# One pool of four PSUM banks in place of three small pools, in a two-layer hybrid streaming trunk on one Trainium2 core

## The chip, the cores and the metric

The kernel runs as one program on one NeuronCore of a Trainium2 chip. The metric is device time in microseconds (us), the median of several executions; lower is better. The engines are named as the profile names them: PE is TensorE (its weight loads are listed apart as PEld), DVE is VectorE, ACT is ScalarE, POOL is GpSimd and SP is SyncE, which issues most of the DMAs. A `q` behind an engine's name means its instruction sequencer.

## The reference

Two layers of a hybrid block work on a prompt of 512 tokens and on a decode group of 32 tokens that share the same weights. Cut to what matters:

```python
h = rms_norm(x, g_mix)
glu_a, glu_b, rq, rk, rv, rg, fq, fk, fv, ff, gates = split_in(h @ w_in)
u = glu_a * sigmoid(glu_b)                                # branch A: causal conv over 31 taps
y_conv = silu(layer_norm(dwconv(up, w_dw_conv) + b_dw_conv)) @ w_conv_out
o, new_ret = retention_chunks(rotary(rq), rotary(rk), rv, ret_state)     # branch B, 8 heads
y_ret = (silu(rg) * group_norm(o)) @ w_ret_out
fq, fk = rms_norm(fq, g_q_fox), rms_norm(fk, g_k_fox)     # branch C, 8 heads of 64
s = fq @ fk.T / 8 + cum_q - cum_k                         # cum: cumulative log forget gate
y_fox = (softmax(where(causal, s, -inf)) @ fv) @ w_fox_out
x = x + (sig(gA) * y_conv + sig(gB) * y_ret + sig(gC) * y_fox) @ w_out
x = x + (gelu(dwconv3(rms_norm(x) @ W_a)) * (rms_norm(x) @ W_b)) @ W_down
```

## The kernel before

All activations are held transposed, 128 channels on the partitions and 544 tokens (32 of the decode group, then 512 of the prompt) along the free side. Every projection is a `gemm` (line 296): eight or more weight blocks of 128x128, streamed from HBM and split by ACT and a POOL-issued DMA into a high and a low part (`Stream.split_part`, lines 201 to 215), are multiplied with two halves of 272 tokens (line 314). A gemm accumulates in one tile `acc` of the pool `psA`, which has two buffers of two banks each, and DVE then evicts it (lines 403, 1040, 1042, 1162, 1203 and others). A new gemm can begin in a bank pair only when the gemm before the last one has been evicted.

The other four banks hold small tiles. Before the change they are three pools: `psS` with two banks (name `s`: scores, head means, sums over channels, transposes of the values), `psT` with one bank (`t`: transposes and the state products of the retention), and `psO` with one bank (`o`: products of probabilities and values). PE writes such a tile, and DVE or ACT reads it out; the bank can be written again when its last reader is done. Nothing else in the change's neighbourhood is shared.

The order of the work is written by hand. A "side" generator (attention in `fox_side`, retention in `ret_side`, group norm in `gn_side`) is advanced at fixed places between the blocks of each gemm (`hook`, `tick`), and the 27 multiply-adds of the depthwise convolution (`conv_side`, line 511, each a DVE instruction of about 0.8 us) are dealt out in the same ticks from `extra`. Each engine executes its instructions in order, so a DVE instruction stands behind the convolution steps that were put ahead of it.

Per layer the sequence is: gates and values of the convolution, q and k of the attention with their head means (`head_mean`, lines 345 and 346, read by `rsqrt`, lines 357 to 362), the value projection with its transposes (lines 648 and 650), then the decode group's scores for two groups of four heads (`s_scores`, line 718, read by DVE at line 729; `s_trans`, line 736, read by ACT at lines 740 and 741), then 16 pairs of prompt scores (`p_scores`, line 771: the even and the odd head's products stand in two `s` tiles and are read by DVE at line 778; softmax at lines 704 to 709; `p_trans`, line 786, read by ACT at line 789; `p_pv`, line 805). The retention follows with five chunks (lines 886 to 939; the state update reads its `t` tile on DVE at line 933 or 937).

Of the kernel before, what the change touches and what calls it, by code (L numbers as in the profile page):

```python
# [11 lines left out]
F32 = mybir.dt.float32  # L12
# [5 lines left out]
P = 128  # L18
# [94 lines left out]
def trunk(ctx, tc, x_in, wpack, wff, consts, params, s_conv, s_ret, s_cache, s_clf, s_ffn,  # L113
          y_out, o_conv, o_ret, o_fk, o_fv, o_lf, o_ffn):
    nc = tc.nc
    PS = bass.MemoryType.PSUM
# [11 lines left out]
    upool = ctx.enter_context(tc.tile_pool(name="upool", bufs=3))  # L128
    dpool = ctx.enter_context(tc.tile_pool(name="dpool", bufs=2, space=bass.MemoryType.DRAM))
    psA = ctx.enter_context(tc.tile_pool(name="psA", bufs=2, space=PS))  # L130
    psS = ctx.enter_context(tc.tile_pool(name="psS", bufs=2, space=PS))
    psT = ctx.enter_context(tc.tile_pool(name="psT", bufs=1, space=PS))
    psO = ctx.enter_context(tc.tile_pool(name="psO", bufs=1, space=PS))

    def Q(dt=F32):
        return qpool.tile([P, 4, T], dt, tag="q", name="q")
# [13 lines left out]
        return ap.rearrange("p (h n) -> p h n", h=2)  # L150

    def psS_t():
        return psS.tile([P, 512], F32, tag="s", name="s")

    def psT_t():
        return psT.tile([P, 512], F32, tag="t", name="t")

    def psO_t():
        return psO.tile([P, 512], F32, tag="o", name="o")


    cst = cpool.tile([P, C_ALL], F32, name="cst")
# [172 lines left out]
    def head_mean(src):  # L335

        hi, lo = Wr(), Wr()
        act(hi, src, AF.Copy)  # L338
        vtt(lo, src, hi.bitcast(F32), op=ALU.subtract)  # L339

        def product():
            res = []
            for h in range(2):
                p = psS_t()[:, :HN]
                mm(p, blkr, half(hi, h), start=True, stop=False)
                mm(p, blkr, half(lo, h), start=False, stop=True)
                res.append(p)
            return res

        return product  # L350
# [13 lines left out]
    class Norm:  # L364
# [26 lines left out]
        def finish(self):  # L391
            self.R = spool.tile([P, T], F32, tag="R", name="R", bufs=1)
            parts = [psS_t()[:, :HN] for _ in range(2)]
            for h, p in enumerate(parts):
                mm(p, ones, half(self.ss, h), start=True, stop=True)
            rsqrt(self.R, parts, D)
# [16 lines left out]
    adma = nc.scalar.dma_start  # L413

    junk = psT_t()
    for _ in range(10):
        mm(junk[:, 0:P], ones, ones, start=True, stop=True)
# [35 lines left out]
    for l in range(DEPTH):  # L453
# [90 lines left out]

        def logf_1():
            t = psT_t()
            for b in range(4):
                nc.tensor.transpose(t[:, b * 64 : b * 64 + 64], zf[0:64, NS + b * P : NS + (b + 1) * P],
# [35 lines left out]
        def logf_2():  # L584
            dma(o_lf[l], LG)
            t = psT_t()
            lg = LG.rearrange("p h b -> p (h b)")
            mm(t[:, 0:56], tri, lg, start=True, stop=True)
            mm(t[:, 64:120], ones, lg, start=True, stop=True)
            tot = t[:, 64:120].rearrange("p (h b) -> p h b", b=NB)  # L590
            pf = spool.tile([P, 8, NB], F32, tag="pf", name="pf", bufs=1)
            nc.vector.memset(pf, 0.0)
            for b in (1, 2, 3, 5, 6):
                vtt(pf[:, :, b], tot[:, :, b - 1], pf[:, :, b - 1], op=ALU.add)
            vtt(CM, t[:, 0:56].rearrange("p (h b) -> p h b", b=NB), pf, op=ALU.add)
# [42 lines left out]
        def v_done(vt, vs, j, out):  # L638
            def done(acc):
                v = Wt()  # L640
                R_norm.evict(v, acc)

                def fin():
                    if out is not None:
                        dma(out[:, j, :], v)
                    t = psS_t()
                    for b in range(4):
                        nc.tensor.transpose(t[:, b * P : (b + 1) * P], v[:, NS + b * P : NS + (b + 1) * P], ident)  # L648
                    s = psT_t()
                    nc.tensor.transpose(s[:, 0:P], v[:, 0:P], ident)  # L650
                    act(vt[:, :, j * P : (j + 1) * P], t.rearrange("p (b n) -> p b n", b=4), AF.Copy)
                    act(vs[0:NS, j * P : (j + 1) * P], s[0:NS, 0:P], AF.Copy)

                after(fin, 2)

            return done
# [22 lines left out]
        def fox_side():  # L679
# [64 lines left out]
            def s_pv(it):  # L744
                g = it["g"]
                pt = it["pt"]
                o = psO_t()
                for pr in range(2):
                    for b in range(3):
                        for e in range(2):  # L750
                            i = pr * 2 + e
                            h = g * 4 + i
                            kk = P if b < 2 else NS
                            vv = vc[:, b, h * 64 : h * 64 + 64] if b < 2 else fvs[0:NS, h * 64 : h * 64 + 64]
                            mm(o[e * 64 : e * 64 + 64, pr * NS : (pr + 1) * NS], vv,
                               pt[0:kk, b * P + i * NS : b * P + (i + 1) * NS], start=(b == 0), stop=(b == 2))
                src = o[:, 0 : 2 * NS].rearrange("p (a n) -> p a n", a=2)
                hl_split(foh[:, 2 * g : 2 * g + 2, 0:NS], fol[:, 2 * g : 2 * g + 2, 0:NS], src)
# [35 lines left out]
            def p_pv(it):  # L794
                h, qb = it["h"], it["qb"]
                if h % 2 == 0:
                    it["mate"]["even"] = it
                    return
                ev = it["even"]
                if qb == 0:  # L800
                    obank[0] = psO_t()
                o = obank[0]
                for b in range(qb + 1):
                    for e, x in ((0, ev), (1, it)):
                        mm(o[e * 64 : e * 64 + 64, qb * P : (qb + 1) * P], fv[:, b, (h - 1 + e) * 64 : (h + e) * 64],  # L805
                           x["pt"][:, b * P : (b + 1) * P], start=(b == 0), stop=(b == qb))
                if qb == 3:
                    hl_split(foh[:, h // 2, NS:T], fol[:, h // 2, NS:T], o)
# [67 lines left out]
        def ret_side():  # L876
# [5 lines left out]
            for c0, c, n in chunks:  # L882
# [25 lines left out]
                yield  # L908
                yield
                o = psO_t()  # L910
                kv = psT_t()

# [408 lines left out]
```

## Time and profile before

| | us |
|---|---|
| median of three runs (1975.41 to 1976.87) | 1976.23 |
| the profiled execution | 1979.67 |
| its span, from the first to the last instruction of the program | 1977.9 |
| PE busy in it | 1944.8 |
| DVE busy | 946.0 |
| ACT busy | 1065.0 |
| POOL busy | 412.6 |

The profiled execution is 3.4 us above the median, and 1.8 us of it lie outside the span. PE is busy in nearly all of it, DVE and ACT in about half, but these are averages over stages: attention and retention lie at about 120 to 345 us in the first layer and 1100 to 1330 us in the second, and the rest is mostly dense gemms.

### The profile page before, as it was taken

To read this page: it belongs to the slowest core of one execution; us is meant where nothing else is said; L and a number is where in the kernel's file an instruction comes from. 1 tells how busy PE (TensorE), PEld (TensorE's weight loads), DVE (VectorE), ACT (ScalarE), POOL (GpSimd) and SP (SyncE) were. 2 spreads that over 40 slices of the span, in tenths; PEclk is the share of its full clock that TensorE was granted. 3 is DMA by queue.
4 is the path that set the end of the run, shared out by engine and by line. 5 is a ranking of instruction groups with operands and counts; after the bars stand their busy time and mean duration, and the time that the engine had idled before them with its cause. 6 is when DMAs were issued, how large, how long until landed. Compare 5 with 4: busy or idle time off the path is not lost.

```text
span 1977.9 us, 37772 instructions
## 1 busy us (share of the span) xinstructions
PE 1944.8 (98%) x15852; PEld 1903.0 (96%) x15852; DVE 946.0 (48%) x1642; ACT 1065.0 (54%) x1467; POOL 412.6 (21%) x573
## 2 busy tenths in 40 slices
PE   9999999999999999999999999999999999999999
PEld 8998899999999999999999987999999999999999
DVE  4486988454334330333225869784534343203320
ACT  7566663665455543455446566536654555434542
POOL 1243422121112221221112343211211122112211
PEclk9999999999999999999999999999999999999999
DMA  8786555667888787888887765647678878877786
GB/s 254 179 208 158 129 129 123 146 156 168 197 195 176 174 177 176 176 175 180 212 203 153 205 145 129 139 110 154 151 176 198 195 174 175 177 177 173 176 182 143
DMA packets 106005, 337.39 MB, mean 171 GB/s; under 512 B 17788, under 2 KB 19436, under 8 KB 105580
## 3 DMA queue, kind: packets, MB, share of 16 engines
q0 software_dynamic: 41616, 151.54, 46.0%
q1 hardware_dynamic: 64076, 183.44, 28.0%
q8 instruction: 124, 2.03, 0.4%
q14 instruction: 45, 0.37, 0.1%
q10 hardware_dynamic: 144, 0.00, 0.0%
HBM read 320.59 MB, written 9.89 MB: 167 GB/s over the span
## 4 chain that ended last, share of the span: by engine, by line
PE 80%; DVE 9%; issue 4%; ACT 4%; DMA 2%; SPq 1%; POOL 1%; DVEq 0%; POOLq 0%; ACTq 0%
PE acc L314 76%; DVE w L511 4%; DMA w<-q 1%; DVE w L778 1%; ACT hi L207 1%; DVE mn L704 1%; ACT lo L210 1%; PE o L805 1%; DVE w L779 1%; SPq L834 0%; DVE q L838 0%; PE s L771 0%; PE t L786 0%; DMA q<-in_wpack_dram 0%; PE s L648 0%
## 5 line engine op out<-in xcount | busy, mean ns | idle before, releaser
L314 PE MATMUL acc<-q,hi 128*128 128x272 f32 x9344 | 1781.7, 290 | 5.6 <-DVE q L333 2.0
L314 PEld LDWEIGHTS acc<-q,hi 128*128 128x128 f32 x9344 | 1470.7, 189 | 19.7 <-issue 7.2
L314 PE MATMUL acc<-q,lo 128*128 128x272 f32 x4672 | 1347.7, 289 | 0.1
L314 PEld LDWEIGHTS acc<-q,lo 128*128 128x128 f32 x4672 | 880.1, 189 | 0.9 <-DMA lo<-in_wpack_dram 0.6
L207 ACT ACTIVATE hi<-raw 128x1024 fp32r<-128x1024 f32 (+1 forms) x292 | 308.7, 1057 | 657.1 <-PE acc L314 656.1
L211 POOL DMA_DIRECT2D lo<-in_wpack_dram x289 | 250.1, 865 | 1273.7 <-ACT lo L210 1236.7
L210 ACT ACTIVATE lo<-hi 128x1024 fp32r<-128x1024 f32 x289 | 304.1, 1052 | 4.5
L511 DVE SCALAR_TENSOR_TENSOR w<-w,par 128x574 f32<-128x574 f32 x208 | 201.2, 967 | 3.7
L1203 DVE TENSOR_TENSOR q<-acc,q 128x544 f32<-128x544 f32 x32 | 23.2, 725 | 218.6 <-PE acc L314 218.6
L403 DVE TENSOR_TENSOR w<-acc,R 128x544 f32<-128x544 f32 x94 | 67.7, 720 | 121.5 <-PE acc L314 119.9
L1162 DVE TENSOR_TENSOR w<-acc,R 128x32 f32<-128x32 f32 x44 | 8.5, 192 | 154.0 <-PE acc L314 153.8
L1170 DVE SCALAR_TENSOR_TENSOR w<-w,par 128x546 f32<-128x546 f32 x44 | 34.7, 789 | 83.5 <-ACT w L1169 83.5
L1172 ACT ACTIVATE w<-w 128x546 f32<-128x546 f32 x44 | 29.1, 662 | 70.6 <-DVE w L1171 70.5
L706 ACT ACTIVATE w<-w,mn 128x128 f32<-128x128 f32 (+4 forms) x68 | 37.8, 556 | 34.9 <-DVE mn L704 31.9
L330 DVE TENSOR_TENSOR q<-w,q 128x544 fp32r<-128x544 f32 x44 | 31.9, 725 | 33.6 <-ACT q L329 33.6
L709 ACT ACTIVATE w<-w,rs 128x128 f32<-128x128 f32 (+4 forms) x68 | 37.8, 556 | 16.8 <-DVE rs L708 16.6
L339 DVE TENSOR_TENSOR wr<-w,wr 128x544 fp32r<-128x544 f32 x24 | 26.0, 1084 | 42.5 <-ACT wr L338 42.5
L518 POOL TENSOR_TENSOR w<-w 128x574 f32<-128x574 f32 x24 | 41.5, 1730 | 17.9 <-ACT w L514 16.5
L1042 DVE SCALAR_TENSOR_TENSOR w<-w,acc 128x544 f32<-128x544 f32 x32 | 23.1, 721 | 43.5 <-PE acc L314 43.2
L361 DVE SCALAR_TENSOR_TENSOR w<-s,w 128x272 f32<-128x272 f32 (+1 forms) x60 | 23.6, 435 | 39.5 <-ACT w L358 39.0
L778 DVE SCALAR_TENSOR_TENSOR w<-ck,CM,s 128x128 f32<-128x128 f32 (+3 forms) x64 | 34.3, 536 | 12.7 <-PE s L771 12.7
L1169 ACT ACTIVATE w<-w,par 128x546 f32<-128x546 f32 x44 | 36.5, 830 | 3.4 <-DVE w L1164 3.4
(206 smaller groups left out, 1414.1 us busy)
## 6 DMA issues: line engine op xcount, KB each, us to landing
raw<-in_wpack_dram SPq DMA_DIRECT2D x290, 512.0 KB, 3.4
lo<-in_wpack_dram POOLq DMA_DIRECT2D x289, 512.0 KB, 5.5
w<-in_x_dram SPq DMA_DIRECT2D x16, 272.0 KB, 4.8
out_dram<-w SPq DMA_DIRECT2D x16, 272.0 KB, 4.5
w<-q SPq DMA_DIRECT2D x64, 68.0 KB, 3.7
ck<-cscr SPq DMA_DIRECT2D x16, 256.0 KB, 4.6
xn<-q SPq DMA_DIRECT2D x8, 272.0 KB, 5.4
w<-xn SPq DMA_DIRECT2D x8, 272.0 KB, 5.8
```

The costliest lines, as they stand in the source:

```text
L207: act(hi[:, sl], self.raw[u][:, sl], AF.Copy)
L210: act(lo[:, sl], hi[:, sl].bitcast(F32), AF.Copy, scale=-1.0)
L211: nc.gpsimd.dma_start(lo[:, sl], wpack[u][:, sl], accum_op=ALU.add)
L314: mm(acc[:, h, :HN], w, half(x, h), start=(i == 0 and j == 0), stop=(i == n - 1 and j == len(passes) - 1))
L403: vtt(two(out), acc, two(self.R), op=ALU.mult)
L511: stt(c, u[:, k : k + CO], pcol(w + k), c, op0=ALU.mult, op1=ALU.add)
L518: gtt(p, p, t, op=ALU.add)
L706: act(L[:, :n], L[:, :n], AF.Exp, scale=-1.0, bias=mn, accum_out=sm)
L709: act(L[:, :n], L[:, :n], AF.Copy, scale=rs)
L778: stt(L[:, :n], c[:, :n], CM[:, h, qb : qb + 1], p[:, :n], op0=ALU.subtract, op1=ALU.subtract)
L1169: act(c, a[:, 0:FO], AF.Identity, scale=pcol(w), bias=pcol(P_FB + j))
L1170: stt(c, a[:, 1 : 1 + FO], pcol(w + 1), c, op0=ALU.mult, op1=ALU.add)
```

## The change

The three pools become one pool `psB` with four buffers, so the number of banks stays at eight. Each small tile takes whichever of the four banks the allocation at build time gives it, instead of a bank of its own kind. No instruction is added or removed.

```diff
     psA = ctx.enter_context(tc.tile_pool(name="psA", bufs=2, space=PS))
-    psS = ctx.enter_context(tc.tile_pool(name="psS", bufs=2, space=PS))
-    psT = ctx.enter_context(tc.tile_pool(name="psT", bufs=1, space=PS))
-    psO = ctx.enter_context(tc.tile_pool(name="psO", bufs=1, space=PS))
+    psB = ctx.enter_context(tc.tile_pool(name="psB", bufs=4, space=PS))
@@
     def psS_t():
-        return psS.tile([P, 512], F32, tag="s", name="s")
+        return psB.tile([P, 512], F32, tag="b", name="s")
     def psT_t():
-        return psT.tile([P, 512], F32, tag="t", name="t")
+        return psB.tile([P, 512], F32, tag="b", name="t")
     def psO_t():
-        return psO.tile([P, 512], F32, tag="o", name="o")
+        return psB.tile([P, 512], F32, tag="b", name="o")
```

The file has two lines less, so a line number of the changed kernel is two below that of before. The order of instructions on POOL and SP is unchanged, on ACT and DVE three and two pairs of neighbours change places, and on PE eight short pieces move by a few instructions. What changes is what PE waits for. First place: PE in the first layer, from the decode scores of the second head group to the first pair of prompt scores, before:

```order
L718 MATMUL s<-q,w 32x256 [waits DVE_49]
L718 MATMUL s<-q,w 32x256 x3
L724 MATMUL s<-w 32x32 [waits Pool_49]
...
L771 MATMUL s<-q 128x256 [waits DVE_49]
L771 MATMUL s<-q 128x256 [waits Activation_49]
L771 MATMUL s<-q 128x256 x4
```

and in the changed kernel:

```order
L716 MATMUL s<-q,w 32x256 [waits Activation_49]
L716 MATMUL s<-q,w 32x256 x3
L722 MATMUL s<-w 32x32 [waits Pool_49]
...
L769 MATMUL s<-q 128x256 [waits DVE_49] x2
L769 MATMUL s<-q 128x256 x4
```

The decode scores of the second group no longer wait for DVE's reading of the first group's scores but for an older ACT copy; the prompt scores behind them now wait for DVE in both banks. Second place: PE in the first layer, where the second decode transposes stand among the second pair of prompt scores, before:

```order
L771 MATMUL s<-q 128x256 [waits DVE_49]
L771 MATMUL s<-q 128x256 x2
L314 MATMUL acc<-q,hi 128x272
L736 MATMUL t<-cst,w 128x128 [waits PE_49,Activation_49]
L737 MATMUL t<-cst,w 128x128
L738 MATMUL t<-cst,w 32x128
L771 MATMUL s<-q 128x256 [waits DVE_49]
L771 MATMUL s<-q 128x256 x2
```

and in the changed kernel:

```order
L734 MATMUL t<-cst,w 128x128 [waits Activation_49]
L735 MATMUL t<-cst,w 128x128
L736 MATMUL t<-cst,w 32x128 [waits DVE_49]
L769 MATMUL s<-q 128x256 [waits DVE_49]
L769 MATMUL s<-q 128x256 [waits DVE_49,PE_49]
L769 MATMUL s<-q 128x256 x4
```

The transposes stand ahead of all six score products, and their bank is another one than that of the first decode transposes. Third place: PE in the retention of the first layer, at its second chunk, where `t` are the transposed keys, before:

```order
L892 MATMUL s<-q 128x128 [waits PE_49] x2
L892 MATMUL s<-q 128x128 x5
L886 MATMUL t<-cst,q 128x128 [waits DVE_49]
L886 MATMUL t<-cst,q 128x128 x3
L892 MATMUL s<-q 128x128
```

and in the changed kernel:

```order
L884 MATMUL t<-cst,q 128x128 [waits PE_49]
L884 MATMUL t<-cst,q 128x128 x3
L890 MATMUL s<-q 128x128
L890 MATMUL s<-q 128x128 [waits Activation_49]
L890 MATMUL s<-q 128x128 x6
```

The transposed keys stand first and no longer wait for DVE.

## Rows read from the trace of the kernel before

**Rows 1.** The page's first lines: span; busy time, share and instructions of each engine.
```profile
span 1977.9 us, 37772 instructions
...
PE 1944.8 (98%) x15852; PEld 1903.0 (96%) x15852; DVE 946.0 (48%) x1642; ACT 1065.0 (54%) x1467; POOL 412.6 (21%) x573
```
**Rows 2.** The page's chain that ended last, shares of the span by line.
```profile
PE acc L314 76%; DVE w L511 4%; DMA w<-q 1%; DVE w L778 1%; ACT hi L207 1%; DVE mn L704 1%; ACT lo L210 1%; PE o L805 1%; DVE w L779 1%; SPq L834 0%; DVE q L838 0%; PE s L771 0%; PE t L786 0%; DMA q<-in_wpack_dram 0%; PE s L648 0%
```
**Rows 3.** Waits of PE, whole span: us in total, times, longest us.
```profile
PE s L771 <- DVE w L778: 4.4, 6, 1.4
PE t L786 <- ACT w L789: 3.9, 5, 1.4
PE s L718 <- DVE w L729: 2.8, 2, 2.4
PE s L345 <- DVE w L361: 2.8, 2, 1.4
PE s L648 <- DVE w L361: 2.8, 2, 2.1
...
PE t L886 <- DVE st L937: 1.9, 4, 0.8
...
PE t L736 <- ACT w L741: 1.4, 1, 1.4
```
**Rows 4.** Stretches in which DVE is full: length, busy us (instructions) by engine, clock, DMA.
```profile
121.00:157.00 36.00, 31.52 (x262) 30.44 (x264) 35.16 (x44) 18.47 (x26) 12.88 (x12) 0.99 0.96 248
...
200.00:249.00 49.00, 43.49 (x351) 38.02 (x348) 47.67 (x87) 31.35 (x65) 20.23 (x15) 1.00 0.52 121
...
1102.00:1139.00 37.00, 33.12 (x262) 31.96 (x264) 36.12 (x45) 18.48 (x26) 12.59 (x12) 0.95 0.85 236
...
1186.00:1231.00 45.00, 41.57 (x336) 36.41 (x334) 45.00 (x84) 28.53 (x60) 16.55 (x14) 1.00 0.55 130
```
**Rows 5.** Stretches of lower granted clock; columns as in rows 4, the clock third from last.
```profile
157.00:160.00 3.00, 3.00 (x25) 2.47 (x22) 1.66 (x6) 2.34 (x7) 0.00 (x0) 0.50 0.88 194
421.00:427.00 6.00, 4.93 (x25) 4.72 (x26) 2.77 (x4) 2.69 (x4) 1.70 (x2) 0.72 0.52 119
1150.00:1153.00 3.00, 3.00 (x13) 2.87 (x13) 1.85 (x5) 1.92 (x7) 1.41 (x2) 0.50 0.90 144
```
**Rows 6.** Timeline, layer one: start us, length us, instruction, [idle before <-releaser].
```profile
149.16 0.72 DVE L403 TENSOR_TENSOR w<-acc,R 128x544 f32<-128x544 f32 x1
...
151.38 0.52 PE L314 MATMUL acc<-q,hi 128*128 128x272 f32 x2
...
156.28 0.51 DVE L729 SCALAR_TENSOR_TENSOR w<-w,cqs,s 128x288 f32<-128x288 f32 x1
...
156.84 1.08 PE L718 MATMUL s<-q,w 64*32 64x256 f32 x8 [2.40 <-DVE w L729]
...
158.09 0.51 DVE L729 SCALAR_TENSOR_TENSOR w<-w,cqs,s 128x288 f32<-128x288 f32 x1 [0.59 <-PE s L724]
...
161.30 0.62 PE L771 MATMUL s<-q 64*128 64x256 f32 x6
```
**Rows 7.** Timeline, the same places in layer two.
```profile
1139.54 0.52 DVE L729 SCALAR_TENSOR_TENSOR w<-w,cqs,s 128x288 f32<-128x288 f32 x1
...
1141.84 0.62 PE L771 MATMUL s<-q 64*128 64x256 f32 x6
...
1147.40 0.33 DVE L778 SCALAR_TENSOR_TENSOR w<-ck,CM,s 128x128 f32<-128x128 f32 x1
...
1149.00 0.33 PE L736 MATMUL t<-cst,w 128*128 128x128 f32 x1 [1.39 <-ACT w L741]
...
1149.48 0.72 PE L771 MATMUL s<-q 64*128 64x256 f32 x3
```
**Rows 8.** Timeline, layer one, end of the full stretch in the attention.
```profile
248.98 0.33 DVE L778 SCALAR_TENSOR_TENSOR w<-ck,CM,s 128x128 f32<-128x128 f32 x1
...
250.28 0.62 PE L771 MATMUL s<-q 64*128 64x256 f32 x6
```

## The prediction, made before the changed kernel was run

> **What bounds the kernel now.** I read the page first. PE is busy for 1944.8 of 1977.9 us [rows 1], so all its idle time is 33.1 us, and a change that adds and removes no instruction can win little more than that. The chain that ended last is mostly PE's gemms, but 4% of it, some 79 us, are the convolution steps of DVE at line 511 [rows 2]. A chain that runs through line 511 says that there are stretches in which DVE, not PE, sets the pace. I then read who waited for whom on PE, to see how much of the idle time is a wait for one of the four small banks, and after that the windows, to see whether DVE was full where these waits stand.
>
> The waits for a small bank's last reader are these [rows 3]: prompt scores 4.4, prompt transposes 3.9, decode scores 2.8, head means 2.8, value transposes 2.8, key transposes of the retention 1.9, decode transposes 1.4. Together 20.0 us, about 1% of the span. PE's other waits are for operands or for the start of the kernel and are not touched.
>
> Four stretches are full on DVE [rows 4]: 35.16 of 36 us from 121 us, 47.67 of 49 from 200, 36.12 of 37 from 1102, 45.00 of 45 from 1186. Each layer has two, one before the attention and one inside it. In such a stretch a PE that no longer waits for one bank runs ahead of DVE and waits for it a little later, so a wait removed there is worth only the distance to the next point where PE needs DVE.
>
> Last, the granted clock [rows 5]. It is 0.50, that is 1.2 instead of 2.4 GHz, from 157 to 160 and from 1150 to 1153 us, right after waits of 2.40 us [rows 6] and 1.39 us [rows 7] for a small bank. From 421 to 427 its mean is 0.72, a loss of 0.28 x 6 = 1.7 us of PE time. I take 1.7 us as the price of one such fall.
>
> **The change, part by part.** The number of banks is the same and every tile still fills one, so no instruction becomes longer. What changes is whose reader a tile waits for. I read the banks that the two built programs assign and ask of each wait in rows 3 which tile now precedes it in its bank, and when the trace shows that tile's last read.
>
> *Head means, value transposes and decode scores, first layer.* In the built program all of them get banks that were read some 7 to 10 us earlier, so their waits of 1.4 (L345), 0.7 (L648, 2.8 less the longest 2.1) and 2.40 us (L718) go. They stand in the first full stretch, though. PE can gain only until it meets the gemm pair: the gemm that begins at 151.38 needs the eviction that began at 149.16 and took 0.72 [rows 6], so its margin is 151.38 - 149.88 = 1.50, and of the first 2.1 us only 1.5 are kept. PE then reaches the second decode group 2.40 + 1.5 us earlier, at 156.84 - 3.9 = 152.9. From there to the first prompt scores it took 161.30 - 156.84 = 4.46 us, about 1.5 of it because of the halved clock (three microseconds at 0.50), so 2.9 us at full clock: it arrives at 155.9. Now it must wait: by the built program the first score bank is the one that DVE reads until 156.28 + 0.51 = 156.79, and the second is that of the second decode group. DVE's read of that one waited 0.59 us for PE [rows 6]; without that it runs from 157.50 to 158.01. So the second score product starts at about 158.1 instead of 161.3: 3.2 us gained if the clock stays up, 3.2 - 1.7 = 1.5 if it falls again, since PE again waits some 2.2 us. Here the stall has moved from line 718 to line 771. Between both ends I take 1.8, near the lower, since the new wait is about as long as the one after which the clock fell.
>
> *The same in the second layer.* The head means, value transposes and decode scores lose their waits (1.4, 2.1, 0.4), but the second prompt score waits for DVE's second read at line 729, which ends at 1139.54 + 0.52 = 1140.06 and starts behind the full stretch, so that it can't move. The score stood at 1141.84 [rows 7]: 1.7 us gained, no more. The decode transposes lose their wait of 1.39 us, but the next score at 1149.48 needs the bank that DVE reads until 1147.40 + 0.33 = 1147.73: again a gain of 1.7 us against before, not a further one. What can come on top is the halved clock of 1150 to 1153 [rows 5], 1.7 us, if the wait that is left doesn't bring it back. The ends are 1.7 and 3.4; I take 2.5, the middle.
>
> *Prompt transposes.* The two long waits of line 786, one per layer (1.2 and 1.4 of the 3.9), end the second full stretch. The transposes get another bank and start at once, but the scores that follow at 250.28 keep their bank's predecessor, which DVE reads until 248.98 + 0.33 = 249.31 [rows 8]: 0.97 us kept, and the same in the second layer, 1.9 together. The other three waits of that group are 1.3 us; some stand in a full stretch. Between 0 and 1.3 I take 0.5.
>
> *Prompt scores.* The 4.4 us stay: in the built program the second head's tile keeps its own bank in these places, and DVE is full there. Between 0 and 4.4 I take 0.
>
> *Retention.* The transposed keys get banks read long before, and nothing on PE's way needs DVE soon after: all of 1.9 us.
>
> Sum: 1.8 + 2.5 + 1.9 + 0.5 + 0 + 1.9 = 8.6 us. After the attention PE is the bound alone, so a lead is kept to the end. The profiled execution of 1979.67 us would become 1971.1; it stands 3.4 us above the median of the runs, and from that median, 1976.23, the forecast is 1967.6 us.
>
> The Trainium skill has a rule for such waits: the page Perfetto Trace Analysis, section Matmuls, says that independent matmul groups should rotate through different PSUM banks so that ACT's or DVE's evacuation of one lies beside the matmuls of the next. By that rule all 20.0 us would go. Rows 4 say why I don't take it: where DVE has no idle time left the reader is late whatever bank it reads.
>
> **The rivals.** *All of it goes.* If DVE's reads move forward with PE also in the full stretches, the 20.0 us go and with them the three falls that follow a bank wait (157, 1150, and one at 1116 behind the longest wait of line 648): 20.0 + 3 x 1.7 = 25 us, 1951 us. For it: PE's waits name banks alone. Against it: rows 4. The rule just named would give this.
>
> *It is swallowed.* The lead is given back in the attention, because DVE and ACT meet it with waits of their own (rotary transfers, softmax), so that only the retention's 1.9 us and one microsecond or so elsewhere remain: 3 us, 1973 us. For it: DVE is full in 45.00 of 45 us [rows 4]. Against it: that stretch is entered through one in which DVE waits for PE, so its start moves with PE.
>
> *Slower.* PE, running ahead, waits in more and differently placed pieces, and the granted clock falls more often; transposes that used to follow an ACT copy now often follow a DVE read in their bank, seven of them per layer in the full stretch of the attention. Each fall costs 1.7 us, so it decides from five extra falls on (8.6 / 1.7); with eight the time is 1967.6 + 13.6 = 1981 us. For it: the clock already falls after waits as short as 1.39 us. Against it: the transposes' new predecessors mostly were read over a microsecond before. The Trainium skill's page TensorE: Matmul & The Clock Gate, section A second HAM failure mode: psum-queue depth-cycling, tells of a kernel whose cycling through PSUM banks made PE idle so often that its clock swung between the two levels; the trace of before shows single falls, not a swing.
>
> **How the numbers follow.** I give the forecast case 0.74, all of it 0.06, swallowed 0.15, slower 0.05. A measurement of this kernel can tell about 0.2%, 4 us, from no change. The forecast case reaches from about 3.3 us (1.5 in the first layer, 1.7 in the second, the rest lost) to 14.7 (the upper ends 3.2 + 3.4 + 1.9 + 1.3 + 1.9 = 11.7, and about three more where the falls near 421 us or their like in layer two don't return). So 1961.5 to 1973.0, which takes in most of the forecast case and of the swallowed one. Faster by over 0.2%: all of it, and most of the forecast case, 0.80. Within 0.2%: 0.15. Slower: 0.05.
>
> **What would show it.** In the changed profile: no wait of PE at lines 343, 646, 716 and 884 (two less than before); waits of one to two microseconds at line 769 before the first prompt scores of each layer, released by line 727; the first layer's first prompt scores at about 158 to 160 us; the waits at line 769 in the full stretches still there, about 4 us; DVE still full there; fewer stretches with the clock at 0.50. The prediction is wrong if line 769's new waits are absent or line 784 waits for DVE line 776 in total for several microseconds, if DVE's L729 runs earlier than 156 us, or if low-clock stretches become more than they were.

## The result, and the profile after

The changed kernel takes 1964.26 us (median), against 1976.55 us for the kernel before on the same chip; the ratio is 0.9931, with a 95% interval of 0.9913 to 0.9948. That is a gain of some 12 to 14 us, within the range that was given, and larger than the 8.6 us that the sum came to. One disturbed execution of the changed kernel (4877.66 us) is left out of the ratio. The profiled execution took 1960.4 us.

The page's first lines, and its chain that ended last by line, after the change (all line numbers are two lower):

```profile
span 1958.5 us, 37802 instructions
...
PE 1934.5 (99%) x15852; PEld 1896.5 (97%) x15852; DVE 944.3 (48%) x1642; ACT 1064.1 (54%) x1467; POOL 414.7 (21%) x573
...
PE acc L312 79%; DVE w L509 2%; DMA lo<-in_wpack_dram 1%; DMA raw<-in_wpack_dram 1%; DVE w L776 1%; PE s L769 1%; ACT lo L208 1%; PE o L803 1%; DVE mn L702 1%; DVE w L777 0%; PE s L890 0%; DMA w<-q 0%; PE o L914 0%; ACT hi L205 0%; PE t L784 0%
```

Against [rows 1], the span is 19.4 us shorter. PE's idle time went from 33.1 us to 1958.5 - 1934.5 = 24.0, and its busy time fell by 10.3 us, although it executes the same instructions: some 5 us of that are three falls of the clock fewer and 1.8 the order in the retention, both below. The convolution steps' share of the chain fell from 4% [rows 2] to 2%. The profiled execution of before stood 3.4 us above its median and this one 3.9 below, so the two profiles overstate what the medians show by some 7 us.

PE's waits after the change, to be read against [rows 3]:

```profile
PE s L769 <- DVE w L776: 5.5, 7, 1.7
PE acc L312 <- DMA lo<-in_wpack_dram: 2.4, 2, 1.6
...
PE s L769 <- DVE w L727: 1.8, 3, 0.8
```

Of the seven groups that waited for a small bank, six are gone: head means, value transposes, decode scores, decode transposes, prompt transposes, key transposes. What is left is the prompt scores' 5.5 us and their new wait of 1.8 us for the decode scores' reader, 7.3 us in place of 20.0.

Windows, columns as in [rows 4]. The four full stretches, moved by the lead, and then the two stretches of lower clock:

```profile
121.00:153.00 32.00, 30.39 (x252) 29.62 (x251) 31.37 (x38) 17.80 (x26) 12.14 (x12) 1.00 0.98 259
...
195.00:242.00 47.00, 43.41 (x361) 38.39 (x356) 46.70 (x85) 30.47 (x64) 20.05 (x15) 1.00 0.56 129
410.00:418.00 8.00, 6.50 (x37) 6.07 (x36) 4.55 (x5) 3.10 (x4) 3.41 (x3) 0.79 0.59 129
1091.00:1125.00 34.00, 33.41 (x288) 32.35 (x286) 33.33 (x39) 20.14 (x29) 14.73 (x14) 1.00 0.96 247
1130.00:1134.00 4.00, 4.00 (x21) 3.94 (x21) 1.93 (x7) 2.76 (x7) 0.81 (x1) 0.58 0.29 72
1171.00:1215.00 44.00, 40.35 (x330) 35.81 (x329) 44.00 (x82) 27.27 (x59) 17.31 (x13) 1.00 0.56 133
```

DVE is as full as before in all four. The clock fell twice while PE was at work, at 1.7 us each (0.21 x 8 and 0.42 x 4). Before it fell five times: the three of [rows 5], and these two in the same view:

```profile
1115.00:1120.00 5.00, 5.00 (x30) 5.00 (x29) 4.96 (x7) 1.38 (x3) 1.96 (x2) 0.66 1.05 268
1405.00:1410.00 5.00, 4.45 (x23) 4.45 (x24) 1.94 (x3) 1.78 (x3) 0.88 (x1) 0.66 0.63 147
```

Timeline, layer one, the places of [rows 6]:

```profile
137.37 0.39 PE L312 MATMUL acc<-q,lo 128*128 128x272 f32 x1 [1.59 <-DMA lo<-in_wpack_dram]
...
149.14 0.72 DVE L401 TENSOR_TENSOR w<-acc,R 128x544 f32<-128x544 f32 x1
...
154.09 0.64 PE L716 MATMUL s<-q,w 64*32 64x256 f32 x8
...
156.25 0.51 DVE L727 SCALAR_TENSOR_TENSOR w<-w,cqs,s 128x288 f32<-128x288 f32 x1
...
157.17 0.38 PE L769 MATMUL s<-q 64*128 64x256 f32 x1
157.39 0.50 DVE L727 SCALAR_TENSOR_TENSOR w<-w,cqs,s 128x288 f32<-128x288 f32 x1
...
157.95 0.62 PE L769 MATMUL s<-q 64*128 64x256 f32 x5 [0.40 <-DVE w L727]
```

The decode scores start without a wait. The first prompt score starts at 157.17 and the second, after 0.40 us of waiting, at 157.95, where all six stood at 161.30. DVE's work has hardly moved there: the eviction that began at 149.16 [rows 6] begins at 149.14, and the read of the first decode scores at 156.25 in place of 156.28. Layer two, the prompt scores of [rows 7]:

```profile
1128.27 0.39 PE L769 MATMUL s<-q 64*128 64x256 f32 x1 [0.64 <-DVE w L727]
1128.85 0.51 DVE L727 SCALAR_TENSOR_TENSOR w<-w,cqs,s 128x288 f32<-128x288 f32 x1
...
1129.41 0.61 PE L769 MATMUL s<-q 64*128 64x256 f32 x5 [0.75 <-DVE w L727]
...
1136.11 0.62 PE L769 MATMUL s<-q 64*128 64x256 f32 x6
```

DVE in the second full stretch, before,

```profile
216.77 0.71 DVE L403 TENSOR_TENSOR q<-acc,R 128x544 f32<-128x544 f32 x1
```

and after, where the second line is to be read against the 248.98 of [rows 8]:

```profile
211.19 0.71 DVE L401 TENSOR_TENSOR q<-acc,R 128x544 f32<-128x544 f32 x1
...
243.41 0.33 DVE L776 SCALAR_TENSOR_TENSOR w<-ck,CM,s 128x128 f32<-128x128 f32 x1
```

Last, PE at the second chunk of the retention in layer one, before:

```profile
313.82 1.16 PE L892 MATMUL s<-q 64*128 64x128 f32 x14
315.75 0.66 PE L886 MATMUL t<-cst,q 128*128 128x128 f32 x4 [0.78 <-DVE st L937]
316.34 0.49 PE L892 MATMUL s<-q 64*128 64x128 f32 x2
316.75 0.52 PE L314 MATMUL acc<-q,hi 128*128 128x272 f32 x2
```

and after:

```profile
306.31 0.60 PE L884 MATMUL t<-cst,q 128*128 128x128 f32 x4
306.83 1.16 PE L890 MATMUL s<-q 64*128 64x128 f32 x16
307.93 0.53 PE L312 MATMUL acc<-q,hi 128*128 128x272 f32 x2
```

From the first of these instructions to the next gemm it was 316.75 - 313.82 = 2.93 us and is now 1.62. Only 0.78 of the 1.31 us is the wait for the bank. The other 0.53 us came with the order: the sixteen score products take less time in one piece than as fourteen and two with the transposes between them. The prediction had priced that order at nothing.

### The profile page after: what moved, and what is told of

Read it like the earlier page. It is cut to its first block, busy times and chain, and to the rows that moved or that the text cites. A ratio compares the mean times of both kernels' runs of the same rounds, so it can differ in the third digit from the quotient of the medians.

```text
span 1958.5 us, 37802 instructions
## 1 busy us (share of the span) xinstructions
PE 1934.5 (99%) x15852; PEld 1896.5 (97%) x15852; DVE 944.3 (48%) x1642; ACT 1064.1 (54%) x1467; POOL 414.7 (21%) x573
## 4 chain that ended last, share of the span: by engine, by line
PE 84%; DVE 6%; DMA 3%; ACT 3%; issue 3%; POOL 1%; SPq 0%; DVEq 0%; POOLq 0%; ACTq 0%
PE acc L312 79%; DVE w L509 2%; DMA lo<-in_wpack_dram 1%; DMA raw<-in_wpack_dram 1%; DVE w L776 1%; PE s L769 1%; ACT lo L208 1%; PE o L803 1%; DVE mn L702 1%; DVE w L777 0%; PE s L890 0%; DMA w<-q 0%; PE o L914 0%; ACT hi L205 0%; PE t L784 0%
## 5 line engine op out<-in xcount | busy, mean ns | idle before, releaser
L509 DVE SCALAR_TENSOR_TENSOR w<-w,par 128x574 f32<-128x574 f32 x208 | 197.2, 948 | 3.7
L707 ACT ACTIVATE w<-w,rs 128x128 f32<-128x128 f32 (+4 forms) x68 | 37.8, 556 | 17.4 <-DVE rs L706 17.3
L516 POOL TENSOR_TENSOR w<-w 128x574 f32<-128x574 f32 x24 | 41.7, 1739 | 17.0 <-ACT w L512 15.2
```

What stands on the lines that cost most here:

```text
L509: stt(c, u[:, k : k + CO], pcol(w + k), c, op0=ALU.mult, op1=ALU.add)
L516: gtt(p, p, t, op=ALU.add)
L707: act(L[:, :n], L[:, :n], AF.Copy, scale=rs)
```

## The experiments

All comparisons are with the kernel before on the same chip. In kernels with two small pools, lines are one below those of before. The first four belong together: the changed kernel again, and the three ways in which two of the three kinds of tile can share while the third keeps what it had.

**The changed kernel again.**

> The changed kernel once more, for a tighter interval and a second profile. Bank theory: the gain is the removed waits for small banks, less what is given back where DVE is full, plus the falls of the clock that go with the waits; it is the same in every execution but for the falls, so 12 to 14 us (ratio 0.9930 to 0.9940), and the second profile shows no wait of PE at lines 343, 646, 716 and 884, two or three stretches at half clock, and a span within about 5 us of the first one's 1958.5. Rival, a chance difference of the two profiled executions: the stage by stage lead of the first profile (3.6 us before the first prompt scores, 2.8 in the attention, 2.5 in the retention of layer one) doesn't come back within 1 us.

Measured: 1966.10 us against 1978.33, ratio 0.9936 (0.9919 to 0.9952). Its profile has the same waits: 6.0 us at line 769 for line 776, 1.6 for line 727, none at lines 343, 646, 716 and 884. Counted from 110 us, its lead over the profile of before is 3.3 us at the first prompt scores (3.6 in the first profile) and grows by 2.3 us in the retention of layer one, as in the first; in the attention between them it grows by 1.8 in place of 3.6, with a fall of the clock at 210 us that the first profile lacks. But for that fall the stages agree to 0.3 us, so the leads of the first profile are no chance. The executions differ in their mean granted clock, and the time goes with it: of before, the lowest clock, 0.994, goes with about 1980 us and the one execution at 1.000 with 1971.4. At the same mean clock, 0.997, three executions of before average 1975.6 us and four of the changed kernel 1965.8, a gain of 9.8 us; the means over all are 0.9957 (20 executions) and 0.9967 (6), which is 0.0010 x 1976 = 2.0 us more. So most of the gain is shorter work and shorter waits, and some 2 us of it are fewer falls of the clock (the clocks are on record to three decimals, 2 us each, so this is a rough division).

**Scores and transposes share three banks, the products with the values keep theirs.**

```diff
-    psS = ctx.enter_context(tc.tile_pool(name="psS", bufs=2, space=PS))
-    psT = ctx.enter_context(tc.tile_pool(name="psT", bufs=1, space=PS))
+    psB = ctx.enter_context(tc.tile_pool(name="psB", bufs=3, space=PS))
     psO = ctx.enter_context(tc.tile_pool(name="psO", bufs=1, space=PS))
```

> Scores and transposes share three banks, the products o keep one of their own. Bank theory: three banks are enough for the tiles in flight, so the waits at the head means, value transposes, decode scores and key transposes go as with four; ratio 0.993 to 0.996, a gain of 8 to 13 us. Rival, the fourth bank is what counts (the bank of o lies free outside attention and retention, and is the one that the head means and value transposes gain): at most 5 us, ratio over 0.9975, with over 4 us of the waits at the head means, value transposes and decode scores (8.4 us before) left.

Measured: 1972.75 us, ratio 0.9982 (0.9967 to 0.9997). PE's waits for small banks in its profile:

```profile
PE s L770 <- DVE w L777: 5.7, 7, 1.7
PE s L717 <- DVE w L728: 3.8, 2, 2.9
...
PE s L344 <- DVE w L360: 2.3, 2, 1.2
PE t L649 <- DVE w L360: 2.0, 1, 2.0
```

The gain is less than the theory gave, and the rival's reading holds: the decode scores, head means and value transposes still wait. With the bank of the products with the values added, in the changed kernel, they go. In the retention the sixteen score products of the second chunk stand in two pieces here, and the scores there take 12.5 us of PE against 10.2 in the changed kernel.

**Transposes and products with the values share two banks, scores keep theirs.**

```diff
     psS = ctx.enter_context(tc.tile_pool(name="psS", bufs=2, space=PS))
-    psT = ctx.enter_context(tc.tile_pool(name="psT", bufs=1, space=PS))
-    psO = ctx.enter_context(tc.tile_pool(name="psO", bufs=1, space=PS))
+    psB = ctx.enter_context(tc.tile_pool(name="psB", bufs=2, space=PS))
```

> Scores keep two banks, transposes and products share two. Bank theory: the waits of the score tiles stay (prompt scores 4.4, decode scores 2.8, head means 2.8, value transposes 2.8 us, within 1.5 us each), the transposes' own (3.9 + 1.9 + 1.4) mostly go; gain 3 to 6 us, ratio 0.997 to 0.9985. Rival, the order of PE's instructions gives the gain and not the waits: the gain follows the order, so if the key transposes stand first as in the changed kernel the retention is as short as there (2.5 us less per layer) and the rest as before.

Measured: 1970.85 us, ratio 0.9963 (0.9949 to 0.9977). The waits at the key transposes and the decode transposes are gone; 3.9 us at the prompt transposes, 2.8 at the head means and 4.1 at value transposes and decode scores stay. In the retention the key transposes stand first in each chunk, as in the changed kernel, and the lead grows there by 2.1 us per layer. So the theory holds for the scores' waits and for two of the transposes' three groups, and the rival for the retention; the gain is above the range that the theory gave.

**Scores and products with the values share three banks, transposes keep theirs.**

```diff
-    psS = ctx.enter_context(tc.tile_pool(name="psS", bufs=2, space=PS))
     psT = ctx.enter_context(tc.tile_pool(name="psT", bufs=1, space=PS))
-    psO = ctx.enter_context(tc.tile_pool(name="psO", bufs=1, space=PS))
+    psB = ctx.enter_context(tc.tile_pool(name="psB", bufs=3, space=PS))
```

> Scores and products share three banks, transposes keep one. Bank theory: the waits of head means, value transposes into s and decode scores go or fall below 2 us in total, those of the transposes (3.9 + 1.9 + 1.4 us) stay; gain 4 to 8 us, ratio 0.996 to 0.998, and together with the case of shared transposes and products the two partial gains add up to about the whole one within 4 us. Rival, the fourth bank for all counts: both partial gains are small, under 2 us each, and don't add up.

Measured: 1971.91 us, ratio 0.9970 (0.9957 to 0.9982). The waits at the transposes:

```profile
PE t L785 <- ACT w L788: 4.5, 5, 1.5
...
PE t L735 <- ACT w L740: 3.3, 2, 2.4
```

As the theory had it, the waits at the value transposes and decode scores are gone, and 2.3 us at the head means are left. The decode transposes wait 3.3 us where before they waited 1.4: PE arrives earlier at the one bank, and part of the lead of 3 to 4 us that it has at the first prompt scores is given back there. In the retention the split order and its wait stand as before, and no lead is added. By the medians the last two kernels gain 7.5 and 6.4 us, 13.9 together, against 12.2 for the change: the scores' part and the transposes' part of the gain roughly add up. The mean clocks differ, though (0.9965 and 0.9976 against 0.9957 of before): at the same clock, 0.997, the two gain 5.2 and 2.5 us, 7.7 together, against 9.8 for the change.

**The order in the retention alone.** The changed kernel with PE's order in each of the ten chunks as it had been before at the second chunk.

```diff
+                for i in range(7):
+                    score(i // 2, i % 2)
                 t = psT_t()
                 for pr in range(4):
                     nc.tensor.transpose(t[:c, pr * P : (pr + 1) * P], rk[:, pr, c0 : c0 + c], ident)
+                score(3, 1)
```

> The changed kernel, with one thing more: in all ten retention chunks PE computes seven of the eight score products, then the four key transposes, then the last score product, which is the split order that stood in the kernel before at its second chunk. Theory (the order of PE's short pieces has a price of its own): without any bank wait the stretch from the first score product of a chunk to the next gemm block gets about 0.4 to 0.5 us longer than in the changed kernel (there 0.90 us at the first chunk and 1.62 us at the second), in ten chunks 4 to 5 us, ratio to the kernel before about 0.996. Rival (only the waits that are gone count, the order costs nothing, as the prediction had it): the stretches stay at 0.9 and 1.6 us and the ratio at 0.9936, the changed kernel's own.

Measured: 1970.01 us, ratio 0.9959 (0.9946 to 0.9972), 3.9 us more than the 1966.10 of the changed kernel. The row that decides is the time in which PE works on the retention's scores alone, with nothing of its waits (windows of that line only; first layer; the busy time of PE and the count stand third): before,

```profile
0.00:990.00 990.00, 6.00 (x80) 4.82 (x80) 1.00 0.76 175
```

after,

```profile
0.00:990.00 990.00, 5.09 (x80) 4.21 (x80) 1.00 0.77 177
```

and with the split order in all chunks,

```profile
0.00:990.00 990.00, 7.24 (x80) 5.49 (x80) 1.00 0.77 176
```

The second layer has the same numbers. So the split costs 2 x (7.24 - 5.09) = 4.3 us in ten chunks, and the time says 3.9; before, where it stood in two chunks of each layer, it cost 2 x 0.91 = 1.8 us. No bank wait is in any of these. Taken from the first score product or transpose to the next gemm, a chunk takes 2.09 us with the split and 1.62 without (the short first one 1.08 and 0.90), which is 4.1 us in ten chunks. The interval of the times alone is wide, some 4 us to either side; the rows decide. The theory holds, and the prediction's "nothing" for the order falls.

**Is it the full DVE that keeps the change from bringing more?** Both kernels with 5 of the 27 convolution steps.

```diff
-                for k in range(27):
+                for k in range(5):
```

> The kernel before, with 5 of the 27 convolution steps of DVE per channel block, which leaves out 22 of the 31 taps of the depthwise convolution: 176 DVE instructions of about 0.8 us fewer, so that DVE isn't full before and in the attention. It is the base for its twin with one pool. Theory (a full DVE is what keeps the change from bringing all the bank waits): some of the bank waits of 20.0 us stay here, and the twin with one pool wins all of what stays, plus the falls of the clock that follow them. Rival (the waits are themselves made by the full DVE): with DVE free less than 8 us of bank waits are left here, the kernel is 10 us or more faster than before, ratio 0.995 or less, and the twin wins less than 8 us.

> The changed kernel with the same 5 of 27 convolution steps (22 of the 31 taps of the depthwise convolution are left out). Theory (full DVE caps the gain): its lead over its twin with three pools is at least the sum of the twin's bank waits on PE, as against 12.7 of 20.0 us with the whole convolution. Rival (the gain is capped elsewhere, by the readers that follow PE itself): it is again some 0.6 of the twin's bank waits, and waits at the prompt scores for the readers of the scores stay at 4 us or more.

Measured: with three pools 1977.34 us, ratio 0.9993 (0.9977 to 1.0009); with one pool 1972.39 us, ratio 0.9970 (0.9955 to 0.9985). PE's longest waits with three pools,

```profile
PE s L771 <- DVE w L778: 7.6, 2, 4.0
PE t L786 <- ACT w L789: 7.0, 9, 2.0
PE s L345 <- DVE w L361: 2.8, 2, 1.4
```

and with one:

```profile
PE t L734 <- ACT w L707: 5.7, 2, 3.1
PE s L769 <- DVE w L776: 4.8, 2, 2.7
PE s L769 <- ACT w L787: 4.3, 6, 1.6
```

Neither theory holds, of the rival only the 4.8 us at the prompt scores. DVE is free (29.08 of the 49 us from 200, where it had 47.67). Four of the seven groups of bank waits are gone with three pools: decode scores, value transposes, key transposes and decode transposes, 8.9 us in [rows 3]. The head means wait as before, and the prompt scores and prompt transposes wait longer, so that 7.6 + 7.0 + 2.8 = 17.4 us are left: a full DVE goes with some of the waits, not with their sum. The clock fell more (a mean of 0.9940 against 0.9961, some 4 us), and the kernel is no faster. The one pool gains 5.0 us by the medians, with some 4 us to either side by the intervals, a smaller part than with the whole convolution, so a full DVE isn't the general cap either. What meets PE here is in the last rows: 5.7 us of waiting for the softmax of the decode group, which is an operand and no bank, and 4.3 us for ACT's reading of transposes, a wait between two kinds of tile that three pools can't have. In this twin much of the lead is swallowed as the second rival had it.

**The convolution dealt out more slowly or faster in the attention**, with one pool (1 or 1.6 per tick) and with three (1 per tick).

```diff
-            extra_n[0] = 1.33
+            extra_n[0] = 1
```

> The changed kernel with the convolution steps dealt out more slowly in the attention, 1 per tick in place of 1.33. Theory (DVE is full in the second stretch of each attention and the remaining waits at the prompt scores for the readers of the scores, 5.5 to 6 us, come from that): these waits fall to 3 us or less and the kernel becomes 2 to 4 us faster than the changed kernel, about 0.992 of before. Rival: the steps put off meet the end of the retention or the drain ahead of the convolution's norm, where PE or DVE then waits for them, and the time is the same or some us longer.

> The kernel before, three pools, with the convolution steps dealt out at 1 per tick in the attention in place of 1.33, the twin of the run with the changed kernel at that pace (0.9997 of before, with two waits of 3.5 us for the copies of the transposed values ahead of the first scores of the retention). Theory (that loss comes from the order of the convolution steps and not from the one pool: with three pools the same bank has the same tile ahead of it): the same waits of about 3.5 us stand here, the kernel is slower than before, ratio 1.005 to 1.008, and its twin with one pool still leads it by 0.5 to 0.8 per cent. Rival (the one pool made the wait): no such wait here, ratio 1.000 or less, so that at this pace one pool brings nothing.

> The changed kernel with the convolution steps dealt out faster in the attention, 1.6 per tick in place of 1.33. Theory (the waits that are left at the prompt scores for their readers come from DVE being full there): these waits rise from 5.5 to 7 us or more, the attention gets longer, and the ratio to before is 0.994 to 0.998. Rival (what counts is where single convolution steps stand ahead of an eviction, not how full DVE is): the waits change places, their sum stays at 4 to 6 us, and the ratio stays at 0.992 to 0.994.

Measured: slower pace with one pool 1977.21 us, ratio 0.9997 (0.9986 to 1.0008); slower pace with three 1989.01 us, 1.0072 (1.0057 to 1.0087); faster pace with one pool 1979.46 us, 1.0026 (1.0012 to 1.0040). The longest waits at the slower pace: with one pool,

```profile
PE s L890 <- ACT q L649: 7.0, 2, 3.5
PE t L784 <- DVE w L776: 4.3, 2, 2.4
```

with three,

```profile
PE s L892 <- ACT q L651: 7.6, 2, 3.8
```

and the longest two at the faster pace with one:

```profile
PE s L769 <- DVE w L776: 8.6, 7, 3.0
PE s L890 <- ACT q L649: 6.7, 2, 3.5
```

The theory for the slower pace fell: the waits at the prompt scores went from 5.5 to 3.4 us, but seven convolution steps came to stand in a row ahead of an eviction of DVE at 302.48 (the first at 293.11; three of them took 1.9 to 2.3 us in place of 0.82, beside POOL's instructions at line 516 from 293.62 to 299.39), ACT's copy of the values behind it came late, and the first scores of the retention waited 3.5 us for it in each layer. In the changed kernel that copy ends at 297.74 and the first scores start at 297.97, so 0.23 us lie between. The waits that came, 7.0 us here and 4.3 of the prompt transposes for line 776, aren't the whole loss. The clock fell more, too: the executions' mean clock is 0.9925, against 0.9967 of the changed kernel, which is 0.0042 x 1976 = 8.3 us of the 11 to 12 by which this kernel is slower than that. The same wait stands with three pools, so the one pool didn't make it, and at this pace one pool is worth 1.0072 - 0.9997 = 0.75%, as much as at the old one, with some 3 us of it the clock (0.9925 and 0.9908). At the faster pace the waits at the prompt scores rose to 8.6 us as the theory had it, but the loss was larger than it said: the wait of 3.5 us came there too, and the mean clock was 0.9928, another 7.7 us against the changed kernel. No pace that was tried beats the changed kernel.

**One pool of three banks.**

```diff
-    psB = ctx.enter_context(tc.tile_pool(name="psB", bufs=4, space=PS))
+    psB = ctx.enter_context(tc.tile_pool(name="psB", bufs=3, space=PS))
```

> The one pool with three banks in place of four, the fourth unused. Theory (sharing and the number of banks both count: sharing two kinds in three banks gave 0.9982 and 0.9970, four banks for all three kinds 0.9936): PE's waits for a small bank come to some 10 to 18 us, between the 20.0 of before and the 7 to 8 of the changed kernel; the retention keeps its new order and gains some 2 us per layer; ratio 0.996 to 1.000. Rival (the kernel never needs four at once, so three shared ones do as well): waits of 7 to 8 us and 0.9936.

Measured: 1980.05 us against 1975.26, ratio 1.0019 (1.0009 to 1.0029). The waits for small banks came to 12.1 us, inside the theory's range and 8 us below those of before, and still the kernel is slower than before, by more than the theory's range allowed, at the same mean clock (0.9960 and 0.9961). The prompt scores alone show most of why (windows of that line, first layer), before,

```profile
0.00:990.00 990.00, 14.10 (x96) 8.23 (x96) 1.00 0.76 175
```

and with three banks:

```profile
0.00:990.00 990.00, 18.35 (x96) 11.16 (x96) 0.99 0.75 174
```

From the same kernel's timeline, one group of six products:

```profile
188.95 0.62 PE L769 MATMUL s<-q 64*128 64x256 f32 x3
...
190.57 0.61 PE L769 MATMUL s<-q 64*128 64x256 f32 x3
```

Six such products took 0.62 us in [rows 6]. Here three take 0.62 and the other three 0.61 a little later. The products of the even and the odd head use different halves of PE's rows (64 of 128) and run together when they stand side by side; in the kernel with three banks gemm blocks stand between them and the pair comes apart (presumably since the second head's tile finds no bank free; that wasn't tried apart). In both layers these products take 36.88 - 28.18 = 8.7 us more of PE's time. The retention's scores come apart at the second chunk as well, 12.5 us against 10.2 in the changed kernel, so the order isn't wholly kept, though the theory had it kept.

The Trainium skill has both halves of this. TensorE: Matmul & The Clock Gate, section Part 3: Packing small matmuls — row/col tiling, says that matmuls in different row groups run at the same time; the 0.62 us for six or for three agree. TensorEngine Tiling (Array Packing), section Gotcha 1: PSUM Pressure, says that different row tiles write to different banks and that this raises the pressure on them; the 14.10 us with the banks of before and the 18.35 with three fit that.

## Why the prediction held, and where its sum was off

The mechanism was right, and the time lies in the range. The terms were too small, and one was missing. The leads here are those of the two profiled executions: by how much the same instruction starts earlier than before.

- **No wait left at lines 343, 646, 716 and 884**: right; the waits of the decode and the prompt transposes for banks are gone as well.
- **First layer, 1.8 us, from 1.5 to 3.2.** The second score product moved from 161.30 to 157.95, 3.4 us, just above the upper end. The step that was mis-sized is the new wait at line 769: 2.2 us were forecast, and it is 0.40, because PE came later. The lead met a weight that wasn't there yet (1.59 us at 137.37), not the eviction that the margin of 1.50 had been worked out for, and the decode scores began at 154.09 and not at 152.9. The clock then stayed up, where the lower end had it fall again. The second product's time, forecast at 158.1, was right to 0.15 us.
- **Second layer, 2.5 us, from 1.7 to 3.4.** The lead grew from 9.3 us (gemms from 477 to 1103 us) to 14.7 (prompt transposes at 1153.8 before, 1139.0 after), by 5.5. Two things were wrong. DVE's second read at line 729, said to be unable to move, ended at 1129.36 in place of 1140.06, 10.7 us earlier where PE had come in with 9.3, so that 3.2 us and not 1.7 were gained at the second score product (1129.41). And the decode transposes' wait of 1.39 us did bring a gain of its own: from there to the prompt transposes the lead grew by another 2.3 us, in which the next six score products stand in one piece at 1136.11 where the transposes had parted them. The clock took no part in that: the fall at 1150 before has its like at 1130 after, and the fall at 1116, which is gone, lies in a full stretch, where its absence made PE earlier but not DVE, for which the scores then waited.
- **Prompt transposes 1.9 + 0.5, prompt scores 0.** The waits of the scores stayed (4.4 before, 5.5 after), as forecast. Over the rest of the two attentions the lead grew by 3.6 and 1.6 us, 5.2 in place of 2.4; in the second execution of the changed kernel, whose clock fell in the first attention, by 1.8 and 1.8.
- **Retention 1.9.** Measured 2.3 us in each layer, 4.5 together. The waits were sized rightly (0.78 at each second chunk); missing was the order, 1.8 us by the rows of the scores alone, and the experiment that puts it back in all chunks shows that it costs by itself. The other 0.8 us are not traced.
- **What limits the gain.** The prediction took less than the 20.0 us because DVE is full in four stretches, where a lead of PE would be stopped. The traces bear that out for the stretches themselves. In the first, DVE does its work at the same times to 0.03 us (149.14 and 156.25), though PE comes 2.75 us earlier to the second decode scores. In the second, DVE is 5.58 us earlier at 216.77 and 5.57 at 248.98; in the third 10.5 at 1116.37 and at 1137.57, while PE, 14.8 us earlier at 1119.8, is down to 12.4 at the second score product; in the fourth 15.2 at 1187.18 and at 1215.85. So DVE's lead grows between the stretches and not in them. It doesn't follow that DVE makes all of the 7.3 us of waits that are left, or that the gain would be larger without it: with DVE emptied it got smaller, since PE then met other things (softmax, the readers of the transposes). What sets the 7.3 us one by one stays open.
- **The signs.** Waits at line 769 of one to two us before the first prompt scores came in layer two (0.64 and 0.75 us) and hardly in layer one (0.40), and the first scores stood at 157.17 and 157.95, a little before the 158 to 160 that were named. The rest came: 5.5 us of waits at line 769 in the attentions, DVE full, fewer falls of the clock, line 727 not before 156 us, and no wait of line 784 for line 776.
- **The rivals.** "All of it" needed 25 us. By the rule of the Trainium skill that was weighed there (Perfetto Trace Analysis, section Matmuls) 20.0 us of waits would go; 12.7 went. "Slower" needed more falls of the clock; there were two in each profiled execution of the changed kernel against five before. The waits between different kinds of tile that it named do occur, but only where the schedule was changed (4.3 us with the short convolution, 4.3 at the slower pace).

The forecast sum of 8.6 us and the order's 1.8 are 10.4 us, against 9.8 at the same mean clock; the clock's 2.0 us make 12.4, against 12.2 by the medians. That this fits so well is in part luck: the 8.6 already hold 1.1 us for the clock (1.8 over 1.5 and 2.5 over 1.7), and in the profiled pair each term came out at about twice its size, 3.4, 5.5, 5.2 and 4.5 us against 1.8, 2.5, 2.4 and 1.9. Of the 7 us by which that pair lies wider apart than the medians, some 3 are falls of the clock (three fewer, at 1.7 us each, against 2.0 us in the mean); where the other 4 come from stays open. The order's part is shown; that the rest of the sum is right term by term is not.

## What to carry to other kernels

Small PSUM tiles that live at different times did better here in one pool than in pools of their own, as long as no bank was given up for it: four shared banks gained 0.6 to 0.7%, three shared by the same tiles lost 0.2%. When the banks of a pool change, compare the order of the instructions on PE too, and price each place where a group of products on half the rows is taken apart: the wait that vanishes is listed in the profile, the lost overlap is not, and shows only as busy time of that line. A lead on PE is worth what the next thing it needs allows, so look there for late operands and weights as well as for the readers of banks. To see whether an engine stops a lead, compare the start of its same instructions in both traces: where the lead of a full engine stays constant through a stretch, that engine sets the pace of the stretch.

## What the hardware showed unexpectedly

Two short waits close together can be followed by half clock, and the same two waits can also pass without it. Two waits of 0.74 and 0.77 us stand at 412.1 and 413.2 us in the changed kernel, and of 0.74 and 0.77 at 415.0 and 416.1 in its second execution. The window around the first pair is the row 410.00:418.00 above, with a clock of 0.79; around the second it is:

```profile
413.00:420.00 7.00, 5.49 (x42) 5.07 (x41) 4.43 (x5) 3.15 (x5) 3.29 (x3) 1.00 0.52 121
```

The clock went from 2.4 to 1.2 GHz in the one (0.21 x 8 = 1.7 us lost) and stayed at 2.4 in the other. So executions of the changed kernel differ by whole falls of 1.7 us, and a pair of profiles can differ by several of them where the medians don't. A fall can also last longer: in the profile at the slower pace with one pool the mean clock from 302 to 312 us is 0.66, which is 3.4 us lost; it fell during the wait of 3.5 us, which ended at 305.37.
